# Two modulation vectors on TensorE and VectorE, a four-tile K lead on two weight rings, and four vectors moved beside the recurrence

## The chip, the core and the metric

The kernel runs on one core of one Trainium2 chip. A core has five engines that run side by side and signal each other by semaphores: TensorE (PE in the profile, with its weight loads as PEld), VectorE (DVE), ScalarE (ACT), GpSimd (POOL) and SyncE (SP), which here only issues DMAs. Each engine takes its own instructions in a fixed order. The metric is the time of one launch on the device in microseconds (us); lower is better.

## The reference

One sequence of 1024 tokens with 1024 features passes through two layers. The first is an RWKV-7 layer (a recurrence over time), the second attends to a shared set of keys and values. Each layer has six modulation vectors, products of one activated conditioning vector with a matrix of 1024 x 6144. What the change touches is the first layer:

```python
c_act = jax.nn.silu(c)
mod = (c_act @ mod_w[i] + mod_b[i])[:, None, :]
sh1, sc1, gt1, sh2, sc2, gt2 = jnp.split(mod, 6, axis=-1)
h = modulate(rms_norm(x, norm_mix_g[i]), sh1, sc1)
...
xr, xw, xk, xv, xa, xg = (h + xx * mu[j] for j in range(6))   # xx: previous token's h minus h
r = xr @ wr
w_log = -softplus(-(w0 + tanh(xw @ w1) @ w2)) - 0.5
k = xk @ wk
v = xv @ wv
a = sigmoid(a0 + (xa @ a1) @ a2)
g = sigmoid(xg @ g1) @ g2
kk = normalized per head(k * k_k)
k = k * (1.0 + (a - 1.0) * k_a)
y = wkv7_scan(r, decay, k, v, -kk, kk * a)     # the recurrence, per head of 64
...
x = x + (1.0 + gt1) * y
h = modulate(rms_norm(x, norm_mlp_g[i]), sh2, sc2)
x = x + (1.0 + gt2) * sq_relu_mlp(h, mlp_up[i], mlp_down[i])
```

So `sc1` and `sh1` are needed before anything is multiplied; `gt1`, `sc2`, `sh2` and `gt2` are needed only behind the recurrence.

## The kernel before

**Tiles.** Features lie on partitions, tokens along the row; the sequence is worked in two halves of 512 tokens. A full product of a half is a stream: 8 out tiles of 128 features, each the sum over 8 input tiles (k). Every input is split in a high and a low part (`xh`, `xl`) and so is every weight (`wh`, `wl`), and a step of a product is three matrix products: high x high (L124), low x high (L126), high x low (L128), 24 for one out tile. `load_w` (L109) loads one out tile's weights into `wraw` (512 KB, on SyncE's queue), ScalarE casts `wh` (L116) and GpSimd subtracts `wl` (L117). The ring `wring` holds two of each. `proj` takes the first `lead` out tiles together, input tile by input tile, and the rest one by one. K's lead is written for four tiles, but the ring has weights for two, and in the trace two tiles run over all input tiles and then the next two.

**Order of the work.** A scheduler takes the instructions as they are written and orders them on each engine; generators (`yield`) interleave the pieces as they are written. `phase_rwkv` first runs the norm of the first half and two modulation vectors (`layer_mod(0, 1)` and `(0, 0)`, through `mod`, L170): for each vector 8 loads `modw` of 128x1024, one VectorE step each that multiplies by a column of `cact` and adds to `modacc` (L180, L182), then 8 one-column products with a vector of ones (L186), which sum over partitions, and the bias (L188). They share the pool `mp`. Then come the h tiles `ha` (L478, L479), and the stream K of half 0 with `lead=4`, beside which the low-rank products for decay and a (`lora_wa`) and the second half's norm run; then R, the gate's low-rank products (`lora_g`) and V. Input tiles are made by `shift` on GpSimd (L658), `mix` on VectorE (L663) and `split` (cast `xh` on ScalarE, `xl` on VectorE, L166 and L167). All short-lived tiles come from one ring `t` of four.

**K's evacuation** (`evac_k`): ScalarE copies the sum from PSUM to `e0` (`kr`, L619) and squares it to `e1` (`kk`, L620); a product with a block matrix sums over heads (L622), then maximum, Ln and Exp (L628, L630, tables loaded for each). With `al`, the last result of `lora_wa` (L562), a product (L635) and a tanh give `at` in `e2` (L636), ScalarE makes the factor for k in `e3` (L638), VectorE multiplies (L637, L639, L640) and three stores follow (L642). Two tiles are worked off together. `e0` and `e1` have two buffers, `e2` and `e3` one.

**The other four vectors** (`mods()`, from a pool `mp2` with five `modw` tiles) are written one step at a time into `rest()`, with `lora_g` and R; the first loads reach SyncE's queue during the K lead.

**The recurrence** (`phase_wkv`) works 16 units of 4 heads x 256 tokens in a chain. `early` and `late` prepare units, `chain` carries the state, with small products and small VectorE steps that wait for one another, and `gate` finishes a unit. Beside the chain `dense` supplies TensorE with work at a set rate: V of half 0, then `lora_wa`, K, V, R and `lora_g` of half 1, then the output product and the MLP of half 0.

## Time and profile before

| quantity | us |
|---|---|
| median of 3 runs | 3409.33 |
| lowest, highest | 3402.66, 3413.01 |
| the profiled execution | 3409.55 |
| its span in the trace | 3407.8 |
| TensorE busy in the span | 3212.7 (94%) |
| VectorE, ScalarE, GpSimd busy | 2092.3, 1431.1, 1368.4 |

The profile is of one execution. A row of a time line has the start, the duration (for merged instructions the whole stretch), the engine, the line of the kernel, the operation with its output and inputs, the count, and in brackets the idle time of the engine just before it with what ended it. One fp32 product shows as two records, so that x16 stands for 8 products. The granted clock (PEclk) is a share of TensorE's full 2.4 GHz; 0.50 is the lower level of 1.2 GHz.

### The profile page before, as it was taken

What the parts mean: (1) busy time and instruction counts of PE and PEld (TensorE: products, weight loads), DVE (VectorE), ACT (ScalarE), POOL (GpSimd) and SP (SyncE); (2) the same over time, 40 slices, a digit from 0 to 9 for tenths busy, and PEclk for the clock granted to TensorE, in tenths of its full rate; (3) what the DMA queues carried; (4) which work ended last, traced back from release to release, by engine and by line L of the source; (5) the groups of instructions that cost most, each with busy time, mean ns of one, the idle gap of its engine ahead of it and who ended that gap; (6) DMA issues with size and microseconds to landing.
All of it is one profiled execution on the core that took longest, in us unless ns stands there. A gap on an engine that the chain in (4) does not pass through costs nothing. (4 is left out here: it accounts for less than half of the span.)

```text
span 3407.8 us, 50293 instructions
## 1 busy us (share of the span) xinstructions
PE 3212.7 (94%) x19108; PEld 2441.4 (72%) x19108; DVE 2092.3 (61%) x3239; ACT 1431.1 (42%) x2284; POOL 1368.4 (40%) x868
## 2 busy tenths in 40 slices
PE   4798999999999998899999999999999999999997
PEld 2466666666777776678878777777778888778886
DVE  7496765666656546377795433555577776455555
ACT  3632236433423223242242556667555454332323
POOL 3464333333433333454434432444433333554444
PEclk7899999899999999999999999999999999999999
DMA  7365344354333225345542233666544442232322
GB/s 270 104 231 154 94 123 139 119 151 143 100 91 106 88 75 177 124 130 173 184 137 95 82 134 115 208 200 182 174 128 138 143 134 95 91 105 99 99 96 84
DMA packets 294064, 452.88 MB, mean 133 GB/s; under 512 B 114720, under 2 KB 170432, under 8 KB 293824
## 3 DMA queue, kind: packets, MB, share of 16 engines
q1 hardware_dynamic: 293824, 449.68, 42.2%
q8 instruction: 151, 2.47, 0.3%
q14 instruction: 89, 0.73, 0.1%
HBM read 371.25 MB, written 78.32 MB: 132 GB/s over the span
## 5 line engine op out<-in xcount | busy, mean ns | idle before, releaser
L117 POOL TENSOR_TENSOR wl<-wraw,wh 128x1024 fp32r<-128x1024 f32 x385 | 951.4, 2472 | 1221.8 <-ACT wh L116 1164.2
L116 ACT CAST wh<-wraw 128x1024 fp32r<-128x1024 f32 x385 | 402.6, 1046 | 709.8 <-PE pk L126 298.2
L124 PE MATMUL pj<-hh,wh 128*128 128x512 f32 x1120 | 449.8, 409 | 9.2 <-ACT wh L116 2.2
L128 PE MATMUL pj<-hh,wl 128*128 128x512 f32 x1120 | 443.2, 401 | 6.0 <-POOL wl L117 6.0
L126 PE MATMUL pj<-hl,wh 128*128 128x512 f32 x1120 | 442.3, 400 | 0.0
L1040 DVE TENSOR_TENSOR mr<-mr 128x512 f32<-128x512 f32 x128 | 276.7, 2163 | 221.5 <-ACT mr L1039 221.3
L1010 DVE SCALAR_TENSOR_TENSOR x<-pj,G,x 128x512 f32<-128x512 f32 x304 | 223.8, 745 | 130.9 <-PE pj L128 129.6
L128 PE MATMUL pk<-hh,wl 128*128 128x512 f32 x688 | 273.5, 404 | 9.7 <-POOL wl L117 9.7
L124 PE MATMUL pk<-hh,wh 128*128 128x512 f32 x688 | 271.5, 400 | 9.7 <-ACT wh L116 6.7
L126 PE MATMUL pk<-hl,wh 128*128 128x512 f32 x688 | 269.4, 398 | 0.0
L124 PEld LDWEIGHTS pj<-hh,wh 128*128 128x128 f32 x1120 | 210.8, 189 | 64.8 <-issue 4.6
L128 PEld LDWEIGHTS pj<-hh,wl 128*128 128x128 f32 x1120 | 210.6, 188 | 59.8 <-POOL wl L117 8.4
L124 PE MATMUL pj<-mh,wh 128*128 128x512 f32 x564 | 237.2, 421 | 17.0 <-DVE x L1010 16.8
L126 PEld LDWEIGHTS pj<-hl,wh 128*128 128x128 f32 x1120 | 210.6, 188 | 47.2 <-issue 2.6
L166 ACT CAST mh<-mr 128x512 fp32r<-128x512 f32 x128 | 79.4, 620 | 372.6 <-DVE mr L1040 206.3
L126 PE MATMUL pj<-ml,wh 128*128 128x512 f32 x564 | 224.4, 398 | 0.0
L1010 DVE SCALAR_TENSOR_TENSOR x<-pk,G,x 128x512 f32<-128x512 f32 x240 | 173.6, 744 | 81.5 <-PE pk L128 81.5
L128 PE MATMUL pj<-mh,wl 128*128 128x512 f32 x564 | 218.6, 399 | 0.0
L182 DVE SCALAR_TENSOR_TENSOR modacc<-modw,cact,modacc 128x1024 f32<-128x1024 f32 x98 | 162.7, 1661 | 39.6 <-DMA modw<-in_modw_dram 26.1
L124 PE MATMUL pk<-mh,wh 128*128 128x512 f32 x460 | 181.4, 396 | 3.5 <-DVE x L1010 3.5
L126 PE MATMUL pk<-ml,wh 128*128 128x512 f32 x460 | 181.3, 394 | 0.0
L128 PE MATMUL pk<-mh,wl 128*128 128x512 f32 x460 | 167.1, 397 | 2.0 <-POOL wl L117 2.0
(333 smaller groups left out, 6502.3 us busy)
## 6 DMA issues: line engine op xcount, KB each, us to landing
wraw<-in_up_dram SPq DMA_DIRECT2D x128, 512.0 KB
wraw<-in_down_dram SPq DMA_DIRECT2D x128, 512.0 KB
modw<-in_modw_dram SPq DMA_DIRECT2D x96, 512.0 KB
wraw<-in_wqg_dram SPq DMA_DIRECT2D x32, 512.0 KB
wraw<-in_wk_dram SPq DMA_DIRECT2D x24, 512.0 KB
wraw<-in_wv_dram SPq DMA_DIRECT2D x24, 512.0 KB
x<-in_xT_dram SPq DMA_DIRECT2D x32, 256.0 KB
wraw<-in_wr_dram SPq DMA_DIRECT2D x16, 512.0 KB
```

The source lines that it names most:

```text
L116: nc.scalar.copy(out=wh, in_=raw)
L117: self.weng.tensor_tensor(out=wl, in0=raw, in1=wh.bitcast(F32), op=ALU.subtract)
L124: mm(out=p, lhsT=wh, rhs=hh[k], start=first, stop=False)
L126: mm(out=p, lhsT=wh, rhs=hl[k], start=False, stop=False)
L128: mm(out=p, lhsT=wl, rhs=hh[k], start=False, stop=last)
L166: self.nc.scalar.copy(out=out_h, in_=src)
L182: nc.vector.scalar_tensor_tensor(out=acc, in0=w, scalar=ck, in1=acc, op0=ALU.mult, op1=ALU.add)
L1010: self.nc.vector.scalar_tensor_tensor(out=x[j][m], in0=ps, scalar=gain[:, m:m + 1], in1=x[j][m], op0=ALU.mult, op1=ALU.add)
L1040: nc.vector.tensor_tensor(out=r, in0=r, in1=r, op=ALU.mult)
```

## The change

The diff makes these edits.

- **Two vectors, `mod_both`.** The first two vectors no longer go through VectorE alone. Of the 8 loads of a vector, the four with even k are folded into `modacc` on VectorE as before; for each odd k TensorE takes the loaded tile itself as the stationary operand and the column of `cact` as the moving one, 8 one-column products. The products over `modacc` are added to the same sums in PSUM.
- **Double weight slots.** `load_w` takes its tiles in turn from the rings in `self.wps`. While the first half's K and R streams and the beginning of V run there are two rings, `wring` and the new `wring0`, so four pairs. `done()` goes back to one ring.
- **K's evacuation.** The K stream of half 0 gets a pool `ev0` with four buffers of `e0` and `e1` and works off four tiles together. In both halves the copy out of PSUM moves from ScalarE to VectorE, and the factor for k from ScalarE to GpSimd. `e2` and `e3` keep one buffer.
- **The other four vectors.** They leave `rest()` and go to `dense()`, one step after every third step of the second half's work beside the recurrence. Their loads are halves (128x512, 256 KB) and take tiles of the ring `t`; the pool `mp2` goes, `modacc` comes from `hp1`.

```diff
     def load_w(self, src, shape=(128, KT, 128)):
-        raw = self.wp.tile(list(shape), F32, name="wraw", tag="wraw", bufs=self.NW[0])
...
+        wp = self.wps[self.nw % len(self.wps)]
+        self.nw += 1
+        raw = wp.tile(list(shape), F32, name="wraw", tag="wraw", bufs=self.NW[0])
...
+    def mod_both(self, src, n0, bcol, out):
+        nc = self.nc
+        mp, bufs, n = self.mod_pool
+        mm = nc.tensor.matmul
+        acc = mp.tile([128, D], F32, name="modacc", tag="modacc", bufs=2)
+        ps = self.small()
+        for k in range(KT):
+            w = mp.tile([128, D], F32, name="modw", tag="modw", bufs=bufs)
+            self.mod_load = nc.sync.dma_start(out=w, in_=src[k * 128:(k + 1) * 128, n0:n0 + D])
+            ck = self.cact[:, k:k + 1]
+            if k == 0:
+                nc.vector.tensor_scalar(out=acc, in0=w, scalar1=ck, scalar2=None, op0=ALU.mult)
+            elif k % 2 == 0:
+                nc.vector.scalar_tensor_tensor(out=acc, in0=w, scalar=ck, in1=acc, op0=ALU.mult, op1=ALU.add)
+            else:
+                if k == KT - 1:
+                    for i in range(8):
+                        mm(out=ps[:, i:i + 1], lhsT=acc[:, i * 128:(i + 1) * 128], rhs=self.cst("ones", 1), start=False, stop=False)
+                for i in range(8):
+                    mm(out=ps[:, i:i + 1], lhsT=w[:, i * 128:(i + 1) * 128], rhs=ck, start=k == 1 and i == 0, stop=k == KT - 1 and i == 7)
...
-                self.drain(self.layer_mod(0, 1))
+                self.layer_mod(0, 1, True)
...
-            self.mod_pool = self.pool(eh, "mp2", side="right"), self.NMW, D
+            self.mod_pool = hp1, 0, HT
+            self.wps = self.wps + [self.pool(eh, "wring0", 3, side="right")]
...
-            k = self.stream(h, 0, 2, xj, ev, al, self.KL)
+            k = self.stream(h, 0, 2, xj, ev, al, self.KL, self.pool(eh, "ev0", 4, side="right"))
...
+        def dense():
+
+            for i, _ in enumerate(half1()):
                 yield
+                if i % 3 == 0:
+                    next(m, None)
             self.drain(m)
...
-            kr, kk = e("e0"), e("e1")
-            S.copy(out=kr, in_=ps)
+            kr, kk = [(ek or ev).tile([128, HT], F32, name=n, tag=n) for n in ("e0", "e1")]
+            V.tensor_copy(out=kr, in_=ps)
...
-            if len(st) < 2:
+            if len(st) < (4 if ek else 2):
...
-                S.activation(out=kp, in_=at, func=AF.Identity, scale=self.kah[:, m:m + 1], bias=self.ka1[:, m:m + 1])
+                G.tensor_scalar(out=kp, in0=at, scalar1=self.kah[:, m:m + 1], scalar2=self.ka1[:, m:m + 1], op0=ALU.mult, op1=ALU.add)
```

How the instructions stand now is shown at three places. The first is SyncE's queue in the opening, behind the first two K weights and the lora weights. `x17` is the last tile of the second half's x, `wraw` a K weight, `modw` a tile of a modulation vector; the number is that of the tile. Before:

```order
L436 DMA x17_732<-in_xT_dram 128x512
L115 DMA wraw_399<-in_wk_dram 128x1024
L177 DMA modw_1164<-in_modw_dram 128x1024
L115 DMA wraw_405<-in_wk_dram 128x1024
L177 DMA modw_1170<-in_modw_dram 128x1024
L177 DMA modw_1176<-in_modw_dram 128x1024
L177 DMA modw_1201<-in_modw_dram 128x1024
L177 DMA modw_1205<-in_modw_dram 128x1024
```

and after:

```order
L460 DMA x17_791<-in_xT_dram 128x512
L117 DMA wraw_753<-in_wk_dram 128x1024
L117 DMA wraw_892<-in_wk_dram 128x1024
L117 DMA wraw_452<-in_wk_dram 128x1024
L117 DMA wraw_464<-in_wk_dram 128x1024
L117 DMA wraw_820<-in_wk_dram 128x1024
L117 DMA wraw_946<-in_wk_dram 128x1024
```

Loads of the third vector are gone from here. `wraw_452` and `wraw_464`, the second and fourth tile of the K lead, lie in `wring0` and stand behind the fifth and seventh tile's (`753`, `892`).

The second place is ScalarE at the end of the K stream, from `al` on. `al` is the copy L562 (L587 after); `e_621`, `e_635` (before) and `e_698`, `e_712`, `e_726` (after) are tanhs of successive tiles, `ka` marks the factor for k, t<-x the squares of the second half's norm. Before:

```order
L562 COPY al<-pk 64x512
L219 ACTIVATE t<-x_728 128x512
L636 ACTIVATE e_621<-pmt,a0h 128x512
L219 ACTIVATE t<-x_729 128x512
L638 ACTIVATE e_622<-e_621,ka_82,kah 128x512
L219 ACTIVATE t<-x_730 128x512
L219 ACTIVATE t<-x_731 128x512
L619 COPY e_648<-pk 128x512
L620 ACTIVATE e_649<-e_648,prm 128x512
L219 ACTIVATE t<-x_732 128x512
L636 ACTIVATE e_635<-pms,a0h 128x512
```

and after:

```order
L587 COPY al<-pk 64x512
L246 ACTIVATE t<-x_788 128x512
L246 ACTIVATE t<-x_789 128x512
L246 ACTIVATE t<-x_790 128x512
L118 CAST wh<-wraw 128x1024
L661 ACTIVATE e_698<-pmt,a0h 128x512
L246 ACTIVATE t<-x_791 128x512
L645 ACTIVATE e_814<-e_813,prm 128x512
L661 ACTIVATE e_712<-pms,a0h 128x512
L645 ACTIVATE e_886<-e_885,prm 128x512
L661 ACTIVATE e_726<-pmt,a0h 128x512
```

The copies out of PSUM and the factors for k are gone from ScalarE, and tanhs stand closer together.

The third place is VectorE in the recurrence, around a unit's state step `st` and the sum `xs`; `sc`, `lb` and `y` belong to the preparation and the gate, `modacc<-t` is a step of a moved vector. Before:

```order
L904 SCALAR_TENSOR_TENSOR st<-pq,pc,sp 128x64
L797 TENSOR_TENSOR sc<-pl,cs 128x4x128 x2
L745 TENSOR_TENSOR lb<-pe,cs 128x512
L886 TENSOR_TENSOR xs<-pq,sc 128x128
L797 TENSOR_TENSOR sc<-pl,cs 128x4x128
L940 TENSOR_TENSOR y<-y,pms 128x512
```

and after:

```order
L929 SCALAR_TENSOR_TENSOR st<-pq,pc,sp 128x64 x2
L184 SCALAR_TENSOR_TENSOR modacc<-t,cact,modacc 128x512
L822 TENSOR_TENSOR sc<-pl,cs 128x4x128 x2
L770 TENSOR_TENSOR lb<-pe,cs 128x512
L965 TENSOR_TENSOR y<-y,pms 128x512
L911 TENSOR_TENSOR xs<-pq,sc 128x128
L822 TENSOR_TENSOR sc<-pl,cs 128x4x128 x2
L918 COPY uv<-pq 64x2x64
```

Between the state step and the next sum there now stands a step of a moved vector.

## Rows read from the trace of the kernel before

**Rows 1.** Busy time by stretch, all engines, with granted clock (PEclk), DMA share and GB/s.

```profile
0.00:52.30 52.30, 15.98 (x48) 10.57 (x48) 33.51 (x44) 18.13 (x25) 10.98 (x24) 0.70 0.88 319
52.30:97.00 44.70, 35.06 (x111) 20.52 (x112) 35.34 (x32) 9.96 (x15) 26.90 (x16) 0.89 0.52 167
97.00:140.00 43.00, 39.24 (x130) 21.53 (x128) 15.05 (x17) 29.02 (x37) 20.97 (x13) 1.00 0.31 103
140.00:170.00 30.00, 16.61 (x23) 6.41 (x23) 19.64 (x29) 26.68 (x37) 8.09 (x8) 0.54 0.35 106
170.00:300.00 130.00, 114.14 (x495) 76.09 (x495) 117.31 (x160) 43.88 (x63) 78.75 (x48) 0.91 0.61 197
300.00:700.00 400.00, 384.10 (x3884) 264.20 (x3884) 257.75 (x589) 172.81 (x272) 143.41 (x124) 0.96 0.43 126
```

**Rows 2.** Time line of all engines, opening: start, us, engine, line, instruction, idle before.

```profile
7.62 8.83 PE L225 MATMUL pms<-t,ones_d 128*128 128x512 f32 x16 [7.62 <-ACT t L219]
...
12.95 0.75 DVE L180 TENSOR_SCALAR modacc<-modw,cact 128x1024 f32<-128x1024 f32 x1 [8.08 <-DMA modw<-in_modw_dram]
...
26.06 3.58 PE L186 MATMUL pmt<-cs,modacc 128*128 128x1 f32 x16 [9.62 <-DVE modacc L182]
...
35.39 6.09 POOL L117 TENSOR_TENSOR wl<-wraw,wh 128x1024 fp32r<-128x1024 f32 x2 [33.32 <-ACT wh L116]
...
35.92 6.64 DVE L182 SCALAR_TENSOR_TENSOR modacc<-modw,cact,modacc 128x1024 f32<-128x1024 f32 x2
...
42.62 3.58 PE L186 MATMUL pms<-cs,modacc 128*128 128x1 f32 x16 [12.98 <-DVE modacc L182]
...
52.33 1.22 PE L124 MATMUL pj<-xh,wh 128*128 128x512 f32 x2 [6.13 <-ACT xh L166]
```

**Rows 3.** Time line of TensorE, the same instructions later, between dense products.

```profile
249.74 1.84 PE L186 MATMUL pms<-cs,modacc 128*128 128x1 f32 x16
```

**Rows 4.** Time line of SyncE's DMA queue, opening.

```profile
6.93 20.09 SPq L177 DMA_DIRECT2D modw<-in_modw_dram  x16
...
36.03 3.90 SPq L436 DMA_DIRECT2D x<-in_xT_dram  x8
```

**Rows 5.** Time line of VectorE, one step of the K lead.

```profile
65.05 1.52 DVE L663 SCALAR_TENSOR_TENSOR t<-t,prm,ha 128x512 f32<-128x512 f32 x1
66.49 0.68 DVE L167 TENSOR_TENSOR xl<-t,xh 128x512 fp32r<-128x512 f32 x1
67.09 1.27 DVE L182 SCALAR_TENSOR_TENSOR modacc<-modw,cact,modacc 128x1024 f32<-128x1024 f32 x1
```

**Rows 6.** Time line of TensorE, K stream.

```profile
97.47 1.02 PE L622 MATMUL pms<-e,cs 128*128 128x512 f32 x2
...
123.39 0.40 PE L128 MATMUL pk<-xh,wl 128*128 128x512 f32 x1
123.63 0.40 PE L124 MATMUL pk<-xh,wh 128*128 128x512 f32 x1
```

**Rows 7.** Time line of ScalarE, end of the K stream.

```profile
119.57 0.58 ACT L562 COPY al<-pk 64x512 f32<-64x512 f32 x1
...
121.37 0.69 ACT L636 ACTIVATE e<-pmt,a0h 128x512 f32<-128x512 f32 x1 [0.68 <-PE pmt L635]
...
128.53 0.69 ACT L636 ACTIVATE e<-pms,a0h 128x512 f32<-128x512 f32 x1 [0.83 <-PE pk L126]
```

**Rows 8.** Time line of TensorE, from K to R.

```profile
136.08 0.49 PE L128 MATMUL pk<-xh,wl 128*128 128x512 f32 x1
...
165.07 0.99 PE L124 MATMUL pk<-xh,wh 128*128 128x512 f32 x1
```

**Rows 9.** VectorE by line and shape, 300 to 700 us: busy, mean ns, idle before.

```profile
L663 DVE SCALAR_TENSOR_TENSOR t<-t,prm,hb 128x512 f32<-128x512 f32 x39 | 38.0, 982 | 4.5 <-POOL t L658 4.4
```

**Rows 10.** VectorE by line and shape, 195 to 290 us.

```profile
L182 DVE SCALAR_TENSOR_TENSOR modacc<-modw,cact,modacc 128x1024 f32<-128x1024 f32 x21 | 36.8, 1754 | 0.1
```

**Rows 11.** TensorE waits, 300 to 700 us: us in total, times, longest.

```profile
PE pj L126 <- DVE xl L167: 8.3, 4, 4.5
```

More of the change, by code (lines that the diff above doesn't have):

```diff
@@ L111, in load_w @@
         nc = self.nc
-        raw = self.wp.tile(list(shape), F32, name="wraw", tag="wraw", bufs=self.NW[0])
-        wh = self.wp.tile(list(shape), F32R, name="wh", tag="wh", bufs=self.NW[1])
-        wl = self.wp.tile(list(shape), F32R, name="wl", tag="wl", bufs=self.NW[1])
+        wp = self.wps[self.nw % len(self.wps)]
+        self.nw += 1
+        raw = wp.tile(list(shape), F32, name="wraw", tag="wraw", bufs=self.NW[0])
+        wh = wp.tile(list(shape), F32R, name="wh", tag="wh", bufs=self.NW[1])
+        wl = wp.tile(list(shape), F32R, name="wl", tag="wl", bufs=self.NW[1])
         self.w_load = nc.sync.dma_start(out=raw, in_=src)
@@ L175, in mod @@
             for k in range(KT):
-                w = mp.tile([128, n], F32, name="modw", tag="modw", bufs=bufs)
+                w = mp.tile([128, n], F32, name="modw", tag="modw", bufs=bufs) if bufs else self.t()
                 self.mod_load = nc.sync.dma_start(out=w, in_=src[k * 128:(k + 1) * 128, n0 + c:n0 + c + n])
@@ L189, in mod, with layer_mod @@
             yield
-    def layer_mod(self, l, j):
+    def mod_both(self, src, n0, bcol, out):
[18 more added lines that the diff above has]
+                    mm(out=ps[:, i:i + 1], lhsT=w[:, i * 128:(i + 1) * 128], rhs=ck, start=k == 1 and i == 0, stop=k == KT - 1 and i == 7)
+        nc.vector.tensor_tensor(out=out, in0=ps[:, 0:8], in1=self.prm[:, bcol:bcol + 8], op=ALU.add)
+    def layer_mod(self, l, j, both=False):
         o = l * 48 + j * 8
+        if both:
+            return self.mod_both(self.ap["modw"][l], j * D, PC[f"modb{l}"] + j * 8, self.md[:, o:o + 8])
         return self.mod(self.ap["modw"][l], j * D, PC[f"modb{l}"] + j * 8, self.md[:, o:o + 8])
@@ L297, in run @@
             self.tp = self.pool(es, "tmp", 4)
-            self.wp = self.pool(es, "wring", 3)
+            self.wps, self.nw = [self.pool(es, "wring", 3)], 0
             self.weng = nc.gpsimd
@@ L401 @@
     NR = 4
-    NMD = 1
     SG = 2
@@ L407 @@
     UC = 10
-    NMW = 5
     NMA = 7
@@ L411 @@
     RP = 0
-    MK = 0
     KA = 16
@@ L506, in phase_rwkv @@
             m = mods()
-            if self.MK:
-                with tc.issue_after(self.w_load.ins):
-                    self.take(m, 2)
             self.beside(second(), k, self.NS)
-            for _ in k:
-                self.take(m, self.MK)
+            self.drain(k)
         r = self.stream(h, 0, 1, xj, ev, al)
@@ L524, in done, with half1 @@
             self.take(v, self.N0)
+            self.wps = self.wps[:1]
             eh.close()
-        def dense():
+        def half1():
             yield from v
@@ L532, in dense @@
             yield from self.lora_g(h, 1, lw)
-        def rest():
-            for _ in self.both(self.lora_g(h, 0, lw), r, 3):
-                self.take(m, self.NMD)
+        def dense():
+            for i, _ in enumerate(half1()):
                 yield
+                if i % 3 == 0:
+                    next(m, None)
             self.drain(m)
-        return rest(), done, dense()
+        return self.both(self.lora_g(h, 0, lw), r, 3), done, dense()
     def both(self, a, b, n):
@@ L579, in lora_g, with stream @@
         nc.sync.dma_start(out=self.gad[:, s], in_=g)
-    def stream(self, h, half, which, xj, ev, al, lead=2):
+    def stream(self, h, half, which, xj, ev, al, lead=2, ek=None):
         nc, ap = self.nc, self.ap
-        V, S, PE = nc.vector, nc.scalar, nc.tensor
+        V, S, G, PE = nc.vector, nc.scalar, nc.gpsimd, nc.tensor
         ident = self.cst("ident")
```

2 lines of the change are left out of this document (1 added, 1 removed).

## The prediction

> **What bounds the kernel now.** I read the stretches first [rows 1]. TensorE is the engine to look at: from 300 us on it is busy for 384.10 of 400 us at a granted clock of 0.96, and no other engine comes near that. So the amount of TensorE work sets the end, and time can be gained only where TensorE stands idle or runs at its lower clock. A rough measure of that loss is the length of a stretch less busy time times granted clock. It gives 44.7 - 35.06 x 0.89 = 13.5 us for 52.3 to 97, 3.8 us for 97 to 140, 30 - 16.61 x 0.54 = 21.0 us for 140 to 170, 26.1 us for 170 to 300 and 31.3 us for 300 to 700. Before 52.3 us there is nothing to multiply: the first product of the K stream starts at 52.33 [rows 2].
>
> Then I read what TensorE waits for in each stretch. At the start it waits for two modulation vectors. Their loads are issued in one run of 20.09 us [rows 4], the first arrives at 12.95, and VectorE folds them into a sum; the last product over that sum ends at 42.62 + 3.58 = 46.2 us [rows 2]. In the K lead VectorE sets the pace: it makes one input tile (1.52 + 0.68 us) and folds in one tile of a later vector (1.27 us), 3.25 us a turn [rows 5], while TensorE needs 6 x 0.24 us for the two out tiles it has weights for [rows 6]. From K to R, TensorE's last K product is at 136.08 and its first R product at 165.07 [rows 8]. In between ScalarE is busy 26.68 of 30 us [rows 1], with the evacuation of K.
>
> **The start.** Eight accumulations of each vector's loads become four on VectorE and four groups of eight one-column products on TensorE, with eight more products over the sum: 2 x (32 + 8) = 80 products against 16. Eight such products take 3.58 us in the two places at the opening [rows 2] and 1.84 us between dense products [rows 3], twice as fast. So the ten groups cost 35.8 us or 18.4 us. TensorE is free for them when the products of the norm end, at 7.62 + 8.83 = 16.5 us [rows 2]. At the fast price TensorE keeps up with the loads, which arrive one every 20.09/16 = 1.26 us, the last at 12.95 + 15 x 1.26 = 31.9; with 3.7 us for the last two groups the vector is done near 36. At the slow price, with the first three groups still fast, it is 16.5 + 3 x 1.84 + 7 x 3.58 = 47. I take the slow one: it is the one measured at this place, and the groups again stand among waits. A second wait follows. Only two of the four weight pairs are in the old ring; the new ring lies in the space of the vectors' pool, so that its two loads stand in SyncE's order behind the loads of x (36.03, 3.90 us, [rows 4]), behind two further weights, and behind the last product on a vector's tile. ScalarE's splits of these two weights stand ahead of its last two h tiles and of all its xh casts. In the fast case the second of these loads lands near 46 and K starts at 48 (4.5 us earlier than now), in the slow case it lands near 51 and K starts at 55.5. Term: **+3 us**, bounds -4.5 and +6.
>
> **The K lead.** Four out tiles take 12 x 0.24 = 2.9 us of each input tile, and VectorE has no vector to fold in (its turn drops from 3.25 to about 2 us), so that TensorE becomes the slower one. It starts at the lower clock, and some twenty products there cost 0.2 us more each, 4 us. With another us for the first weight after the lead, 5 us of the 13.5 remain. Term: **-9 us**, bounds -5 and -12.
>
> **K to R.** The evacuation of K's tiles runs through one e2 and one e3 buffer: tanh, the k' factor, two products on VectorE, two stores, and only then the next tanh. From one tanh to the next it takes 128.53 - 121.37 = 7.2 us [rows 7]. The copies out of PSUM go to VectorE and the k' factors to GpSimd, eight instructions each off ScalarE for this half; with four pairs of e0 and e1, four tiles leave PSUM before al is ready, and their Ln and Exp are done ahead of it. Between al and the first R cast ScalarE has 47 instructions in its order before the change, 8 of them table loads, and 36 with 6 table loads after. The k' factor can now stand behind one weight split on GpSimd, up to 3 us [rows 2]; the next tanh and all ScalarE work behind it wait for that. Five tanhs, so four turns of 6 to 7 us, and the rest make 31 us from al to the first R product, against 165.07 - 119.57 = 45.5 now [rows 7, 8]. But TensorE has by then done nearly all small products of the tail, some 13 pieces of about 1 us [rows 6], and with three R weights ready its R lead is dense. Term: **-14 us** here, bounds -3 and -18, and **-5 us** in the first 20 us of R, where two thirds of K's tail stands now, bounds 0 and -9.
>
> **V.** The 32 accumulations of the other four vectors, 512 KB each, leave this part of the program: 21 of them take 36.8 us of VectorE between 195 and 290 us [rows 10], a stretch in which VectorE is busy 117.31 of 130 us [rows 1]. What is late next is the input tiles of V and the small steps of the second unit on VectorE, and the weights. Of the 26.1 us that TensorE loses from 170 to 300, some 20 lie behind K's tail, and I take half of them back. Term: **-10 us**, bounds 0 and -20.
>
> **The recurrence.** The four vectors come back as 64 loads of 256 KB into the ring of four t tiles and 64 steps of 128x512 on VectorE, one at every third step of the second half's streams, in with the chain's own small instructions. The nearest instruction is a 128x512 step of two operands at 982 ns in this stretch [rows 9]: 64 x 0.98 = 63 us, and 8 copies of K's second half add 5. VectorE goes from 257.75 to some 326 of 400 us. Behind each such step waits at most a step of the chain, and behind that TensorE, which now waits for VectorE 8.3 us in four waits at most [rows 11]. An accumulation whose load is late would also hold the chain. SyncE's queue gets 64 loads that may have to wait for a free t; behind them stand weights and the recurrence's own small loads. If TensorE's other work covers it all, it costs nothing; if half of the 68 us comes through, 34. I take **+9 us**, nearer to zero because TensorE has dense products to do between the chain's. One thing weighs against it: when VectorE and GpSimd work side by side they stretch each other, 6.64 us for two accumulations of 1.27, and 6.09 for two GpSimd splits [rows 2, 5]. With GpSimd busy 143.41 of 400 us [rows 1] that is in the 982 ns. The Trainium skill (SBUF — State Buffer, section on SBUF's two separate sides) says that the two share one port pair as an exclusive lock, so that the one that comes second is blocked for the whole instruction. By that rule I estimate 64 x 0.36 x 1.5 = 35 us of blocking, half a split at each meeting; the rows give 64 x (0.98 - 0.68) = 19 us, and the sum would be some 2 us higher by the rule.
>
> **Sum.** +3 - 9 - 14 - 5 - 10 + 9 = -26 us, against the profiled execution's 3409.55 us (span 3407.8): 3383.5. The median of the runs shown is 3409.33, so nothing has to be shifted. A difference of 0.3%, 10 us, is about what a measurement of this kernel can tell from none.
>
> **Rivals.** First, more is gained: the opening stays at the full clock (-4.5 in place of +3), V's stall goes altogether (-20 in place of -10), and dense products cover all of the moved steps (0 in place of +9): 26.5 us less, 3357. For it speaks that TensorE runs at full clock in the norm just ahead; against it the two 3.58 us rows [rows 2].
>
> Second, the evacuation stays as it is: the single e2 and e3 buffers still give a turn of 7.2 us, the tanhs wait for the stores, and the first R cast, which stands behind the fifth tanh, comes 45 us after al as now. Then -14 and -5 go, and -7 us are left: 3402.5, which counts as no change. For it speaks that this loop is not touched by the change; against it that ScalarE itself is 89% busy there and loses work.
>
> Third, on the other side: VectorE becomes the bound of the recurrence. It runs in order, so that a chain step stands behind every moved step, its load and every meeting with GpSimd. If all 68 us come through to TensorE, the time is 3383.5 - 9 + 68 = 3442. It decides for slower from the point where TensorE's added waits between 300 and 700 us exceed the 35 us gained before; now its largest wait there is 8.3 us in total [rows 11], and against it speaks that VectorE would still be idle for a fifth of the time.
>
> **Chances.** Forecast 0.58, more gained 0.17, evacuation unmoved 0.15, VectorE the bound 0.10. The range holds the forecast with its bounds, most of the first rival and most of the second: 3355 to 3405. Faster by over 0.3% (below 3399): 0.58 less 0.03 for its slow edge, 0.17 and a little of the second rival, 0.05, together 0.77; within 0.3%: 0.14; slower: 0.09.
>
> **What would show it.** In the changed kernel's trace the product groups over the vectors should take 3.6 us each from the third or fourth on and K should start near 55; if they take 1.8, K starts near 48. The K lead should show some 12 products per input tile with no wait of over 0.5 us, the fourth tile ending about 26 us after the first product. From al to the first R product I look for 31 us, and between tanhs for 6 to 7. Between R and the recurrence VectorE should have gaps. In the next 400 us after it, VectorE should be busy near 80%, with TensorE's waits on it up by about 10 us. The forecast is wrong if K to R stays over 42 us, or if TensorE's idle time in the recurrence grows by over 30.

## Result, and the profile after

The changed kernel takes 3444.12 us, the median of 4 runs (3441.05 to 3456.44), beside 3409.14 us (3402.66 to 3413.01) for the kernel before in the same session: a ratio of 1.0115, with a 95% interval of 1.0095 to 1.0134. It is 35 us slower, where 26 us less was forecast. (The ratio is not the quotient of the two medians, which is 1.0103.) The profiled execution's span is 3442.7 us.

The stretches of [rows 1] with the opening's end moved to the new start of K; columns as there.

```profile
56.40:97.00 40.60, 39.81 (x139) 25.02 (x140) 33.16 (x31) 15.86 (x20) 29.42 (x20) 0.95 0.18 58
97.00:140.00 43.00, 33.70 (x103) 16.94 (x101) 18.33 (x19) 22.21 (x29) 23.55 (x15) 0.90 0.39 126
140.00:170.00 30.00, 16.73 (x19) 5.22 (x20) 18.54 (x28) 23.22 (x31) 5.93 (x8) 0.50 0.26 91
170.00:300.00 130.00, 117.08 (x551) 77.03 (x549) 90.89 (x144) 37.82 (x56) 70.22 (x52) 0.95 0.47 145
300.00:700.00 400.00, 362.56 (x3499) 246.01 (x3500) 294.80 (x608) 153.07 (x238) 149.22 (x124) 0.93 0.49 145
```

Length less busy time times clock, as in the prediction, gives 2.8, 12.7, 21.6, 18.8 and 62.8 us. Before it was 13.5, 3.8, 21.0, 26.1 and 31.3. So the K lead lost 10.7 us less, the stretch behind it lost 8.9 us more, 140 to 170 stayed as it was, 170 to 300 got 7 us back, and 300 to 700 loses 31.5 us more, although VectorE is busy for only 74% of it.

The opening on TensorE, which answers to [rows 2] and [rows 3] (two records are one product):

```profile
15.78 1.62 PE L213 MATMUL pmt<-cact,modw 128*128 128x1 f32 x14
24.41 3.55 PE L211 MATMUL pmt<-cs,modacc 128*128 128x1 f32 x16
31.23 10.38 PE L213 MATMUL pms<-cact,modw 128*128 128x1 f32 x48
44.89 3.55 PE L213 MATMUL pms<-cact,modw 128*128 128x1 f32 x16
56.45 1.22 PE L126 MATMUL pj<-xh,wh 128*128 128x512 f32 x2 [8.01 <-ACT xh L168]
```

The first group is fast, the later ones take 3.55 us each, and K starts at 56.45. TensorE has no gap from 7.04 to 48.44 us; its granted clock is 1.00 up to 17.0, 0.65 in the mean from there to 24.4, and 0.50 from 24.4 on, the lower of its two levels. From `al` to R on ScalarE (compare [rows 7]; L661 is the tanh, L168 the first cast for R):

```profile
122.41 0.59 ACT L587 COPY al<-pk 64x512 f32<-64x512 f32 x1
126.71 0.69 ACT L661 ACTIVATE e<-pmt,a0h 128x512 f32<-128x512 f32 x1 [0.23 <-PE pmt L660]
136.22 0.69 ACT L661 ACTIVATE e<-pms,a0h 128x512 f32<-128x512 f32 x1 [2.66 <-DMA bd<-e]
141.94 0.69 ACT L661 ACTIVATE e<-pmt,a0h 128x512 f32<-128x512 f32 x1 [1.47 <-DMA bd<-e]
149.49 0.69 ACT L661 ACTIVATE e<-pms,a0h 128x512 f32<-128x512 f32 x1
166.23 0.67 ACT L661 ACTIVATE e<-pms,a0h 128x512 f32<-128x512 f32 x1
168.07 0.62 ACT L168 CAST xh<-t 128x512 fp32r<-128x512 f32 x1
```

From `al` to R's first cast are 45.7 us; before it was 163.12 - 119.57 = 43.6 us, and the fifth tanh came behind that cast:

```profile
163.12 0.60 ACT L166 CAST xh<-t 128x512 fp32r<-128x512 f32 x1
166.98 0.69 ACT L636 ACTIVATE e<-pms,a0h 128x512 f32<-128x512 f32 x1
```
R's first product on TensorE, to which the forecast of 31 us ran, comes later still, behind small products that follow the cast:

```profile
172.96 0.80 PE L126 MATMUL pk<-xh,wh 128*128 128x512 f32 x1
```

That is 172.96 - 122.41 = 50.6 us from `al`, against 45.5 before. The four turns from the first tanh to the fifth take 9.5, 5.7, 7.6 and 16.7 us. Two of the tanhs wait for a store of `e`, the single e2 buffer. From `al` to the cast, before and after (columns as in [rows 1]; ScalarE is the fourth engine):

```profile
119.57:163.12 43.55, 28.95 (x72) 14.14 (x72) 21.11 (x29) 36.21 (x48) 15.83 (x13) 0.74 0.33 111
122.41:168.07 45.66, 23.09 (x39) 8.11 (x37) 21.52 (x33) 27.39 (x38) 12.82 (x13) 0.60 0.28 95
```

ScalarE's work fell by 8.8 us, from 36.2 to 27.4, and the time in which it stood idle grew by 10.9, from 7.3 to 18.3. VectorE in the same stretch (time, duration, then idle time ahead and its releaser):

```profile
129.86 1.74 DVE L664 TENSOR_TENSOR e<-e,e 128x512 f32<-128x512 f32 x1 [14.72 <-POOL e L663]
132.12 0.68 DVE L644 COPY e<-pj 128x512 f32<-128x512 f32 x1
137.82 0.69 DVE L664 TENSOR_TENSOR e<-e,e 128x512 f32<-128x512 f32 x1 [5.02 <-POOL e L663]
```

VectorE stands 14.72 us in front of L664, which needs the factor from GpSimd (L663), which needs the tanh, which needs `al`; the tanh ends at 127.40, but the factor starts at 129.05, behind a weight split of 2.35 us on GpSimd. The copies out of PSUM (L644), taken from ScalarE, now stand behind L664 in VectorE's order, and ScalarE waits 10.6 us for them in three waits (120 to 170 us, ahead of the squares of L645). So ScalarE lost work there and gained waits.

In the recurrence, the largest waits of TensorE from 300 to 700 us (us in total, times, longest); before they came to 16 us in all:

```profile
PE pq L925 <- DVE st L929: 8.8, 4, 5.3
PE pq L925 <- DVE uv L918: 4.5, 5, 1.9
PE pq L894 <- DVE st L929: 4.3, 1, 4.3
```

The moved steps in VectorE's groups of the same stretch, and SyncE's longest waits ahead of their loads (L179), 37.8 us in these three rows:

```profile
L184 DVE SCALAR_TENSOR_TENSOR modacc<-t,cact,modacc 128x512 f32<-128x512 f32 x48 | 40.7, 848 | 11.9 <-DMA t<-in_modw_dram 11.6
L182 DVE TENSOR_SCALAR modacc<-t,cact 128x512 f32<-128x512 f32 x7 | 7.1, 1020 | 0.2 <-DMA t<-in_modw_dram 0.2
```

```profile
SPq L179 <- DVE xl L169: 15.3, 4, 7.0
SPq L179 <- DVE tm L791: 13.7, 4, 6.2
SPq L179 <- DVE t L688: 8.8, 5, 4.2
```

### The profile page after: what moved, and what is told of

The parts are those of the page before. It is cut to its first block, busy times and chain, and to the rows that moved or that the text cites. A ratio compares the mean times of both kernels' runs of the same rounds, so it can differ in the third digit from the quotient of the medians.

```text
span 3442.7 us, 50625 instructions
## 1 busy us (share of the span) xinstructions
PE 3253.6 (95%) x19236; PEld 2472.5 (72%) x19236; DVE 2108.3 (61%) x3283; ACT 1410.5 (41%) x2250; POOL 1373.7 (40%) x884
## 5 line engine op out<-in xcount | busy, mean ns | idle before, releaser
L168 ACT CAST mh<-mr 128x512 fp32r<-128x512 f32 x128 | 79.4, 621 | 373.8 <-DVE mr L1065 203.6
L130 PEld LDWEIGHTS pk<-hh,wl 128*128 128x128 f32 x688 | 132.3, 192 | 46.4 <-POOL wl L119 15.8
```

The lines of the kernel that those rows point to most:

```text
L130: mm(out=p, lhsT=wl, rhs=hh[k], start=False, stop=last)
L168: self.nc.scalar.copy(out=out_h, in_=src)
```

## A ruler along the recurrence

The scan over time (L735, L760 after) runs once in each unit, in the same sequence in every kernel. Its start on VectorE's time line, less that of the kernel before, shows where a kernel wins or loses (first line: before, in us; the rest: difference to it).

```
scan                1st     3rd     6th     9th    10th    13th    16th
before            173.3   340.0   479.2   657.8   703.3   874.7  1094.5
changed            +2.7   -11.7    +5.3   +13.2   +28.0   +35.7   +35.5
e2_move            -8.1   -20.4   -12.4    -3.1    -0.9    +8.4   +10.7
e10_before_out     -7.2   -25.6   -25.7   -30.8   -30.1   -30.1   -30.2
e3_out             +2.2   -15.9   -15.8   -10.3    -8.7    -8.2    -8.2
e20_out_open       +1.6   -19.2   -19.2   -14.8   -12.7   -12.5   -12.3
```

The changed kernel is 11.7 us ahead at the third scan, 28.0 behind at the tenth and 35.7 at the thirteenth. The moved steps run from 266 to 708 us, from ahead of the third scan to ahead of the tenth. The 7.7 us between the tenth and the thirteenth are lost behind the last of them; without the vectors (e3_out) nothing is lost there, and their cause stays open. Each line is one execution, and it ends at the sixteenth scan: behind it the profiled executions of the experiments below differ by another 12 us less to 6 us more, which the ruler does not show.

## Experiments

Each was timed against the kernel before on its chip. Differences in the text are (ratio - 1) x 3407 us, 3407 being about the kernel before, so that runs of different sessions can be set side by side; the intervals make each uncertain by 4 to 11 us. The quotients of the medians give differences that lie up to 6 us from these (the changed kernel +35, e8_open +34, e7_steps +19).

```
run                    median us   ratio to before, 95%        difference
changed kernel          3444.12    1.0115 (1.0095-1.0134)       +39
e2_move                 3425.56    1.0053 (1.0036-1.0071)       +18
e3_out                  3403.00    0.9992 (0.9978-1.0006)        -3
e10_before_out          3386.82    0.9934 (0.9914-0.9953)       -22
e6_loads                3419.69    1.0037 (1.0023-1.0051)       +13
e7_steps                3422.62    1.0073 (1.0042-1.0105)       +25
e14_phase               3440.69    1.0091 (1.0075-1.0107)       +31
e22_queue               3448.02    1.0131 (1.0116-1.0145)       +45
e8_open                 3438.20    1.0085 (1.0063-1.0106)       +29
e20_out_open            3400.22    0.9982 (0.9964-0.9999)        -6
e21_out_open_evac1      3400.53    0.9975 (0.9960-0.9989)        -9
e9_evac1                3439.92    1.0093 (1.0068-1.0118)       +32
e4_two                  3415.97    1.0033 (1.0022-1.0045)       +11
e11_before_two          3425.14    1.0044 (1.0028-1.0060)       +15
e18_out_two             3400.77    0.9976 (0.9963-0.9988)        -8
e19_out_two             3400.72    0.9974 (0.9960-0.9989)        -9
e12_both                3424.98    1.0053 (1.0036-1.0071)       +18
e17_three               3424.77    1.0054 (1.0034-1.0074)       +18
e23_later               3398.70    0.9988 (0.9975-1.0001)        -4
```

### What the four vectors cost, in the old place and in the new

**e2_move**: the kernel before, with `mods()` taken out of `rest()` and put at every third yield of `half1()`, its loads in `self.t()`.

> The kernel before with one part of the change alone: the four later modulation vectors leave the stretch beside R and V and come back as 64 loads of 256 KB into the t tiles, each with one VectorE step, beside the recurrence; opening, K lead and evacuation as before. Theory M (the moved vectors cost the recurrence some 47 us, since the changed kernel is 11.7 us ahead at the third scan of the recurrence and 35.7 us behind at the thirteenth): R and V win some 8 us, the recurrence loses 47, 3445 to 3450 us. Rival N (the loss comes from the other parts, such as K's second half evacuated by VectorE and GpSimd, and the moved vectors are covered): 3395 to 3405 us.

**e3_out**: the changed kernel without the vectors.

```diff
-                for i in (2, 3, 4, 5):
-                    yield from self.layer_mod(0, i)
+                V.memset(self.md[:, 16:48], 0.0)
+                yield
```

> The changed kernel with the four moved vectors left out (their 64 loads, 64 VectorE steps and 32 one-column products; the vectors are set to zero). Theory M: the 47 us of the recurrence go, 3395 to 3400 us. Rival N: what costs the time is elsewhere, 3435 us or more. Between them, the part of the 47 us that the vectors explain can be read off.

**e10_before_out**: the same edit in the kernel before.

> The kernel before with the four later modulation vectors left out (set to zero; their loads, VectorE accumulations and products are gone). With the changed kernel without them at 3403 us, this gives what the rest of the change (opening, K lead, evacuation) is worth by itself. Theory A (the vectors cost some 20 us where the kernel before had them, since the kernel with the move alone is 20.4 us ahead at the third scan, and the rest of the change costs 15 to 20): 3380 to 3388 us. Rival B (the vectors were covered beside R and V, and the rest of the change is worth nothing either way): 3400 to 3406 us.

The three make a square. Without the vectors the kernel before is at -22 and the changed one at -3; with them they are at 0 and +39; the move alone is at +18. So the vectors cost 22 us beside K, R and V, and 42 us (39 + 3) or 40 us (18 + 22) in the recurrence, whichever kernel they stand in. The rest of the change costs 19 us without them and 21 with them. Theory M holds in kind; for e2_move its 47 us were too many, since 8.4 + 20.4 = 29 us of them are lost by the thirteenth scan. Theory A of e10_before_out holds. The old place was not free, but in these kernels the new one costs twice as much. That price is not fixed: with the opening undone the moved vectors cost 35 us (29 + 6, e8_open and e20_out_open), and with the second tanh buffer described below 20 (11 + 9, e4_two and e19_out_two), while the old place costs 23 with such buffers (15 + 8, e11_before_two and e18_out_two). So 42 us is what they cost in the layout of the changed kernel.

### Loads or steps

**e6_loads** leaves out the later seven steps of each half vector, **e7_steps** the later seven loads (`w = acc` in their place), **e14_phase** has `if i % 3 == 1`, and **e22_queue** issues the loads with `nc.scalar.dma_start`.

> The changed kernel with 56 of the 64 VectorE steps of the moved vectors left out (the loads into the t tiles stay, and the first step of each half vector). Of the 41 us that the moved vectors cost, theory V (VectorE's time: 56 steps of 0.74 to 0.85 us and the chain's steps behind them) gives back most: 3405 to 3415 us. Rival Q (SyncE's in-order queue, which waited some 47 us for free t tiles ahead of these loads between 300 and 700 us, with weights and the recurrence's reloads behind): still 3430 to 3440 us.

> The changed kernel with 56 of the 64 loads of the moved vectors left out; the 56 VectorE steps stay, in the same places, and fold the sum into itself (same shape, no load to wait for). Of the 41 us of the moved vectors the loads alone cost 17 (the kernel with loads and without steps, 3420 against 3403 without either). Theory V+Q (loads and steps cost apart and add up): the steps alone 24, 3424 to 3430 us. Rival W (a step costs mainly because it waits in VectorE's order for its load): near 3403 to 3412 us.

> The changed kernel with each step of the moved vectors one place later in the second half's streams (the same work, loads and spacing; 460 of 3285 places in VectorE's order differ). Theory V or Q (the moved work costs its time wherever it stands): 3440 to 3450 us. Rival R (where the steps fall against the recurrence's chain decides, as with a chain step behind a step that waits for its load): a change of over 10 us, either way.

> The changed kernel with the 64 loads of the moved vectors issued on ScalarE's queue in place of SyncE's. Theory Q (the 17 us of the loads are SyncE's in-order queue, which waits for a free t tile with the recurrence's reloads behind): 10 to 17 us less, 3427 to 3434 us. Rival T (the loads cost by holding t tiles that shifts and mixes need, whatever queue issues them, or the wait now holds ScalarE): 3440 to 3450 us.

Against -3 without the vectors, the loads alone cost 16 us, the steps alone 28 (20 by the medians), both 42: about a sum. So steps and loads each have a price, where V and Q each gave all of it to one of them, and W falls. The phase makes no difference that can be told (8 us, with overlapping intervals), so R falls for this one shift: the work costs in both places. On ScalarE's queue the loads are not cheaper, so the forecast of Q for e22_queue fails. That does not clear an in-order queue of the cost, since the wait went along: ScalarE's own waits that end with a moved load or with a step of `modacc` come to 16.1 us there in seven rows, against 1.2 in the changed kernel (300 to 700 us). The longest:

```profile
ACT L952 <- DMA t<-in_modw_dram: 4.4, 1, 4.4
```

What the loads do shows also on VectorE, which waits for the reload of the small blocks: in the kernel without vectors, with loads alone, and with the loads on ScalarE's queue (300 to 700 us); with the steps alone there is no such wait, and it is 2.8 us in the kernel before and 8.7 in the changed one:

```profile
DVE tm L791 <- DMA lblk<-Ld: 1.8, 2, 1.2
```

```profile
DVE tm L791 <- DMA lblk<-Ld: 11.6, 4, 4.2
```

```profile
DVE tm L791 <- DMA lblk<-Ld: 9.1, 3, 4.5
```

Whether the 256 KB loads delay that reload on the DMA engines, or the t tiles that they wait for and hold delay what stands ahead of it, stays open.

### Opening, K lead and evacuation

**e8_open** calls `self.drain(self.layer_mod(0, 1))` and the same for vector 0, as before. **e20_out_open** is that without the four vectors. **e21_out_open_evac1** adds, for the second half, K's copy and factor on ScalarE as before; **e9_evac1** has this last edit alone, in the changed kernel.

> The changed kernel with the opening undone: the first two vectors by eight VectorE accumulations each, as before. Theory O (the one-column products at the slow price and the later weights cost the start 4 us, and nothing downstream takes it up): K starts near 52.3 in place of 56.45, 4 us less, 3440 us. Rival P (VectorE and the weight ring of the K lead set the pace after, so that the start does not matter): within 2 us of 3444.

> The changed kernel without the four moved vectors (set to zero) and with the opening undone; what is left of the change is the K lead and the evacuation. Beside 3403 us (opening changed) and 3387 us (nothing changed), both without the vectors. If parts add up without the vectors: 6 us less than with the changed opening, 3397 us, and K lead with evacuation cost 10 us. If lead and evacuation cost nothing by themselves: 3387 to 3390 us.

> The same without vectors and with the opening undone, and K's second half evacuated as before too; what is left is the K lead and the first half's evacuation. Theory K2 (the second half's copies and factors on VectorE and GpSimd cost 10 us): 3387 us. Rival K1 (the first half's lead and evacuation cost it): as without this edit, 3397 us.

> The changed kernel with K's second half evacuated as before (copy and k' factor on ScalarE); the first half as changed. Theory K2 (the eight copies on VectorE and eight factors on GpSimd between 526 and 676 us cost the recurrence 10 us: without any moved vectors, the kernel with the rest of the change loses 11.1 us against the kernel before between the seventh and the ninth scan): 3432 to 3437 us. Rival K1 (the first half's lead and evacuation cost it, and the second half is covered): 3441 to 3447 us.

The opening costs 10 us with the vectors and 3 without, both within their intervals of the 4 us by which K starts later. K lead and evacuation, with the second weight ring that no run takes out by itself, cost 16 us without vectors and opening (-6 against -22), and undoing the second half leaves 13 of them; in the changed kernel that edit gives 7, which the intervals do not tell from nothing. So K2 falls, and most of the cost goes with the edits to the first half. ScalarE's copy `al` in e20_out_open and in e10_before_out, both starting K between 52 and 53:

```profile
121.09 0.58 ACT L587 COPY al<-pk 64x512 f32<-64x512 f32 x1
```

```profile
111.88 0.58 ACT L562 COPY al<-pk 64x512 f32<-64x512 f32 x1
```

With four out tiles in the lead, `al` comes 9.2 us later: the last small products that it needs (L584) are issued among the dense products of four tiles and end at 120.4, against 111.1 with two. The first scan follows `al` by nearly the same time in both, 53.7 and 54.2 us (before 53.7, changed 53.6, e2_move 53.9), and comes 8.8 us later than in e10_before_out; R's first cast comes 5.3 us later. The other half of the 16 us comes between the sixth and the ninth scan; its cause stays open, since undoing the second half's evacuation did not remove it.

### A second tanh buffer

**e4_two**: in the changed kernel every other tile's tanh lies in the first half's own pool, and k' is written over K's copy, from where it is stored. The accumulator of the moved vectors goes to a pool of its own to make room, so that what e4_two gains belongs to both edits.

```diff
-                a2, at, kp = ev.tile(..., name="a2", tag="a2"), e("e2", 1), e("e3", 1)
+                a2, at, kp = ev.tile(..., name="a2", tag="a2"), (ek if ek and m % 2 else ev).tile([128, HT], F32, name="e2", tag="e2", bufs=1), e("e3", 1)
...
-                V.tensor_tensor(out=kp, in0=kp, in1=kr, op=ALU.mult)
+                V.tensor_tensor(out=kr if ek else kp, in0=kp, in1=kr, op=ALU.mult)
```

**e11_before_two** alternates e2 and e3 between two places in the first half of the kernel before; **e18_out_two** and **e19_out_two** are e11_before_two and e4_two without the vectors. **e12_both** is e4_two with the opening undone, **e17_three** that with e9_evac1's edit.

> The changed kernel with a second buffer for K's tanh (e2) in the first half, and k' written over K's own copy, so that neither tanh nor factor waits for a store; the accumulator of the moved vectors lies elsewhere to make room. Theory E (the turn of 7 us from one tanh to the next, set by the single buffers and the stores, keeps R's first cast 45.7 us behind al): turns of 3 to 4 us, al to first R cast 31 to 35 us, 8 to 12 us less than the changed kernel, 3432 to 3436 us. Rival S (ScalarE's own order with its six table loads sets it): al to first R cast over 42 us, 3440 to 3446 us.

> The kernel before with the tanh and factor buffers of K's first half (e2, e3) alternating between two places; nothing else. Theory E (the single buffers hold ScalarE and R's first cast by the stores): al to first R cast falls from 43.6 us to below 36, 3392 to 3400 us. Rival S (what gained 28 us in the changed kernel with two buffers was mostly another order in the recurrence, not the evacuation: its first R cast came 45.9 us after al as before): al to first R cast stays over 41 us, and the time moves by less than 8 us, either way.

> The kernel before without the four vectors (set to zero) and with the alternating tanh and factor buffers that made the kernel before 18 us slower. Theory H (the buffers themselves cost: tanhs in pairs hold ScalarE and R): 3400 to 3405 us against 3387. Rival R (the 18 us come from how the vectors' steps and the recurrence's fell into another order): 3383 to 3391 us.

> The changed kernel without the four vectors (set to zero) and with the second tanh buffer that made the changed kernel 28 us faster. Theory E (the buffer itself is worth it): 3375 to 3385 us against 3403. Rival R (it came from another order of the moved vectors' steps and the recurrence): 3398 to 3406 us.

> The changed kernel with the opening undone and with the second tanh buffer in K's first half. If the 28 us and the 6 us that these gave one at a time add up: 3410 us. If the 28 us came from how the recurrence's work happened to be ordered, and not from the evacuation: 3425 to 3440 us.

> The changed kernel with the opening undone, the second tanh buffer in K's first half, and K's second half evacuated as before. If all three add up with 10 us for the last: 3400 us, below the kernel before. If the order rather than the parts decides: between 3410 and 3440 us.

ScalarE in e4_two, `al`, two tanhs, and R's first cast:

```profile
121.59 0.58 ACT L587 COPY al<-pk 64x512 f32<-64x512 f32 x1
127.00 0.68 ACT L661 ACTIVATE e<-pms,a0h 128x512 f32<-128x512 f32 x1
136.66 0.69 ACT L661 ACTIVATE e<-pmt,a0h 128x512 f32<-128x512 f32 x1 [8.98 <-DMA bd<-e]
167.50 0.61 ACT L168 CAST xh<-t 128x512 fp32r<-128x512 f32 x1
```

The tanhs come in pairs, and the cast still comes 45.9 us after `al`. But the wait for a store did not go, as the expectation had it: the third tanh alone waits 8.98 us for one, where the changed kernel waited 4.1 us in two. What the gap is without that wait is shown in e11_before_two and e18_out_two, where no tanh waits for a store: 47.8 and 46.4 us. In the first of them, from `al` to the cast:

```profile
120.03:167.84 47.81, 35.53 (x79) 18.05 (x80) 25.73 (x35) 43.42 (x59) 17.13 (x14) 0.70 0.36 124
```

ScalarE is busy for 43.4 of these 47.8 us. So theory E falls for the gap, and in the kernel before S, ScalarE's own order, holds; in the changed kernel the two are not told apart. Neither has the times: e4_two gained 28 us, more than both forecasts, and e11_before_two lost 15, where S allowed 8. The same idea that gained 28 us here cost the kernel before 15 us, 14 us of it without the vectors, gave 6 in the changed kernel without them, 11 with the opening undone (e12_both against e8_open), and nothing adds up in e17_three. So I find no price of the buffer by itself. What fits all six runs is that the order of the whole recurrence is planned anew with each edit, and that this moves the time by 15 us and more either way; it is not shown by a run in which the order alone differs by so much (e14_phase, where it alone differs, moved by 8 us). The time of e18_out_two is the one that theory H forecast, that of e19_out_two the one of rival R. But H's mechanism, that tanhs in pairs hold R, is not what e18_out_two shows: its first cast for R comes at 157.68, 3.9 us ahead of e10_before_out. e18_out_two is 27.0 us ahead of the kernel before at the second scan, 11 more than without the buffer, and then loses 17 us to e10_before_out between the ninth and the tenth scan, with the same work to do. That stretch in e10_before_out, and in e18_out_two:

```profile
627.00:673.00 46.00, 44.07 (x495) 32.32 (x494) 30.73 (x80) 17.07 (x28) 15.07 (x14) 1.00 0.45 136
```

```profile
625.00:688.00 63.00, 56.69 (x513) 40.93 (x514) 37.06 (x85) 19.72 (x34) 17.35 (x16) 0.81 0.41 121
```

TensorE idles 6.3 us in place of 1.9, and its granted clock falls to 0.81. A second such place is shown below, under the hardware.

### A version with the vectors later, not elsewhere

**e23_later**: the kernel before with one edit.

```diff
+            first = self.w_load.ins
             for _ in self.both(self.lora_g(h, 0, lw), r, 3):
-                self.take(m, self.NMD)
+                with tc.issue_after(first):
+                    self.take(m, self.NMD)
```

> The kernel before with one edit: the loads of the four later vectors are issued only after the first weights of R, so that none of their VectorE steps stands in the K lead; the first vector's steps now stand between K and R, where VectorE is busy 13.7 of 40 us, the rest beside R and V. Theory L (the vectors cost 8 us in the K lead, al at 119.6 against 111.9 without them, and the gap behind K is free): 3397 to 3402 us, under the kernel before. Rival C (R and V get what the lead is spared: with the vectors VectorE is busy 107 of 120 us from 180 to 300): 3404 to 3412 us.

It took 3398.70 us against 3404.66 in its session, 0.9988 (0.9975 to 1.0001): better than the changed kernel by 43 us, and against the kernel before just short of what can be told from no change. `al` comes at 112.53 in place of 119.57, the eight steps of the first later vector stand on VectorE between 133 and 156, behind the lead, and yet the first scan is where it was (+0.3 us): it follows `al` by 61.0 us here, not by 54. The kernel is 8.7 us ahead at the second scan, 2.1 at the third and level at the ninth, so R and V take back what it gains, and the 4 us by which it is faster in the median are not explained by the ruler. No version with the vectors beats the kernel before beyond doubt.

## Why the prediction was wrong, step by step

- **The start, +3: right in size, not in its reason.** K started at 56.45 where 55.5 was forecast, the late groups took 3.55 us where 3.58 was read. I expected the slow price because the groups would stand among waits; the profile shows no gap among them, and the granted clock was 0.50 all the same. Undoing it gave 10 us with the vectors and 3 without; the 4 us lie within both.
- **The K lead, -9: right in its stretch, wrong in the sum.** TensorE's loss there fell from 13.5 to 2.8 us, and it waited at most 0.5 us. But the next stretch starts from `al`, and `al` came at 122.41 in place of 119.57. Without the vectors a lead of two tiles brings it at 111.88 (e10_before_out). The step that failed is to count a denser stretch as a gain without asking whether what ends it, the small products ahead of `al`, comes sooner.
- **K to R, -14, and R, -5: wrong; the second rival was nearer.** From `al` to R's first product 31 us were forecast and 50.6 measured, 5 more than before; the rival had it unchanged, at 45 (it names R's cast, but 45.5 was the time to R's product; to the cast it was 43.6). I counted what leaves ScalarE, and that did leave: 8.8 us. The term that failed is the waits. A tanh waits for the last one's factor, products and stores, and moving work to VectorE and GpSimd put two more in-order queues into that circle, so that ScalarE stood idle for 18.3 us in place of 7.3. The four turns were counted at 6 to 7 us each from one turn of 7.2; they took 39.5 us in all, and before the change 166.98 - 121.37 = 45.6.
- **V, -10: too small for what left, and half of it kept.** The stretch from 170 to 300 lost 18.8 in place of 26.1 us, 7 us less, where V and the term for R together had 15. Taking the vectors out of the old place is worth 22 us (e10_before_out), more than this term and that of the lead together.
- **The recurrence, +9: wrong, the term that decides.** It is +31.5 us by the stretch from 300 to 700 and 42 us by e3_out. The steps were sized near enough (55 of them took 40.7 + 7.1 us, 0.87 each, where 0.98 was read); what failed is how much of them TensorE's other work covers. Of the 63 us forecast for them 20 to 28 came through, and the loads, which I had named and given no price, cost 16 of their own. VectorE never became the bound (74% busy), so the third rival had the time, 3442, by luck: it lets all 68 us come through and keeps 35 us of gains, and neither was so. What it says of order, that a chain step stands behind a moved step, its load and a meeting with GpSimd, is what the rows show, as short waits in the chain and not as a full engine. TensorE's idle time in the stretch grew by 21.5 us (37.4 against 15.9), and the other 10 us of the loss are the lower clock (0.93 against 0.96), which the term had left out. The bound of +34 was too low, and the other gains could not pay for it. Of the two signs of being wrong that the prediction named, K to R over 42 us was there, and 30 us more idle time in the recurrence was not.
- **The sum by the experiments**: the vectors leave, -22; they come back, +42; opening, lead and evacuation, +19: +39. It has to come out, since the three are the steps of one path from the kernel before to the changed one (e10_before_out and e3_out between them); what it shows is the size of each step. Of the forecast's -35 us of gains only the 22 of the vectors' leaving are there, and the rest of the change costs 19. The second rival with this price in it, 3402.5 - 9 + 42 = 3435.5, comes near by errors that offset each other: it has -16 for the start, the lead and V, where the runs have +19 and -22.

## What to carry to other kernels

Moving work off a busy stretch is priced by its cost at the new place, with its loads and not only its steps: here the same four vectors cost 22 us in one place and 42 in the other, and 20 in the other when a buffer was added as well. A stretch that becomes denser gains nothing if the value that the next stretch starts from comes no sooner; look for that value (here `al`) first, and remember that it may not be enough, as e23_later shows. Count waits as well as work when instructions move from one in-order engine to two others. Where a planner lays out the whole program anew with each edit, one edit here gave 28 us in one kernel and cost 15 in the other, so test an edit in more than one setting before giving it the credit.

## What the hardware showed that I had not expected

One short wait of TensorE cost almost twice its length. The changed kernel from 688 to 708 us, in stretches of 4 us (columns as in [rows 1]):

```profile
688.00:692.00 4.00, 2.22 (x24) 1.41 (x20) 2.66 (x4) 2.02 (x3) 2.35 (x2) 1.00 0.78 237
692.00:696.00 4.00, 0.48 (x3) 0.36 (x4) 3.93 (x7) 0.00 (x0) 2.33 (x2) 0.88 0.32 114
696.00:700.00 4.00, 4.00 (x21) 2.35 (x22) 2.57 (x8) 0.00 (x0) 0.84 (x1) 0.50 0.09 29
700.00:704.00 4.00, 4.00 (x56) 3.23 (x53) 1.86 (x10) 0.37 (x1) 0.00 (x0) 0.50 0.83 236
704.00:708.00 4.00, 4.00 (x41) 3.31 (x39) 2.66 (x8) 0.48 (x2) 0.00 (x0) 0.84 0.49 188
```

TensorE is idle for 1.78 + 3.52 = 5.3 us, and then busy at the lower clock for 8 us and at 0.84 for 4: another 4 + 0.6 us of its work are lost, 9.9 us for a wait of 5.3. That the wait brought the lower clock is read from the order of the rows; no run takes out this wait alone. What it waited for, on VectorE and GpSimd:

```profile
689.63 0.18 DVE L791 TENSOR_TENSOR tm<-lblk,ti 64x28 f32<-64x28 f32 x1
689.85 2.23 DVE L792 TENSOR_TENSOR ti<-ti,tm 64x28 f32<-64x28 f32 x1
692.11 2.27 DVE L791 TENSOR_TENSOR tm<-lblk,ti 64x39 f32<-64x39 f32 x1
694.31 0.73 DVE L184 SCALAR_TENSOR_TENSOR modacc<-t,cact,modacc 128x512 f32<-128x512 f32 x1
695.18 0.28 DVE L929 SCALAR_TENSOR_TENSOR st<-pq,pc,sp 128x64 f32<-128x64 f32 x1
```

```profile
689.65 4.67 POOL L119 TENSOR_TENSOR wl<-wraw,wh 128x1024 fp32r<-128x1024 f32 x2 [10.02 <-PE pj L130]
```

Two VectorE steps that take 0.2 us in the median took 2.23 and 2.27 us, each the length of one of GpSimd's two weight splits (4.67 / 2 = 2.33 us); behind them stood a moved step of 0.73 us, and only then `st`, for which TensorE waited. The Trainium skill (SBUF — State Buffer, section "SBUF: two separate sides") says that of a VectorE instruction with two inputs in SBUF and a GpSimd one that reads SBUF the one that starts second is blocked for the whole of the first, and these rows agree. Such a meeting is not new in itself: in the kernel before the longest of these steps (L766) took 2.43 us. The prediction set that rule at 2 us over the rows' price; it spoke of the moved steps alone, and here it was the chain's own small steps that were blocked.
